# SyncE's order around the overflow branch, and how the expert rows come back into h at the end of each layer

## The chip, the cores and the metric

The kernel runs on one core of a Trainium2 chip. The metric is the device time of one execution in microseconds (us), the median of three runs. The engines are TensorE (PE, with its weight loads as PEld), VectorE (DVE), ScalarE (ACT), GpSimd (POOL) and SyncE (SP), which computes nothing and issues most transfers. Each engine runs its instructions in the order of the program; engines wait for each other and for transfers by semaphores.

## What is computed

Two layers over 512 tokens and 16 meta tokens, 1024 wide, in float32. In each layer projections feed two groups of attention heads, and a mixture of 32 experts follows, of which each token takes two. The change lies in the experts and at the layer's end:

```python
for l in range(DEPTH):                       # 2
    proj = h @ w_in[l]
    ...                                      # two head groups -> mix
    h = layer_norm(DEEPNORM_ALPHA * h + mix, ln1_g[l], ln1_b[l])
    ffn = hier_moe(h, w_grp[l], b_grp[l], w_rtr[l], b_rtr[l], w1[l], w3[l], w2[l])
    h = layer_norm(DEEPNORM_ALPHA * h + ffn, ln2_g[l], ln2_b[l])
# in hier_moe, with combine = the gate of a token for an expert, 0 where not taken:
hid = silu(einsum('td,edf->tef', t, w1)) * einsum('td,edf->tef', t, w3)
y = einsum('tef,efd->td', hid * combine[..., None], w2)
```

## The kernel before

The 528 tokens of h lie in SBUF as tiles of 128 rows, t1 to t4, and the 16 meta tokens as tile 0 (`mq`). In the traces and orders one buffer `hu` holds t1 and t2 of h, and a second one t3 and t4.

**The expert loop.** The 32 experts run as 16 pairs. A pair has six weight parts of 1 MB, four of w1 and w3 and two of w2 (`load_part`, line 311), which SP's queue loads into buffers of one rotating pool, the units. SP's transfers share eight semaphores in rotation, so a transfer waits until the one eight before it has landed. For a pair POOL gathers the rows of its tokens (xe, line 1239), PE transposes them (xtq, line 1368), ACT and DVE write them as xT (lines 1375 and 1373), PE multiplies by w1 and w3 (h, 32 matmuls), ACT and DVE make hid (lines 1322 to 1324), PE transposes it (hidT) and multiplies by w2 (yp, 16 matmuls), ACT and DVE scale yp by the gates (yw, lines 1353 and 1354), and POOL scatters yw into a table in memory, `ytab` (line 1576). The table has two halves, one for each of a token's two experts. Pairs 14 and 15 are not scattered: their rows reach h by matmuls with a selection matrix (cmb, in `combine`).

**The branch.** Ahead of pair 8 stands `overflow()`, a branch (line 1413) for experts with more tokens than their place holds. It is taken in neither layer here. Every engine passes it; SP waits there until all its transfers have landed, and POOL until all of its own have. The loop asks SP for the weights of pairs 8, 9 and 10 ahead of the branch; the units that are free allow it pair 8, pair 9 and four parts of pair 10.

**The next layer's small loads.** `begin(l + 1)` makes six loads of 0.5 to 144 KB (`gw`, `lcol`, `ng`, `alog`, `dtb`, `br`). In layer 0 it is called behind the branch. Two small operations read them soon: `eal` on ACT (line 418, from `alog`) and `hng` on DVE (line 504, from `ng`).

**The end of a layer.** In pair 15, `fetch_rows` adds the two halves of ytab to h: for each of t1 to t4 one accumulating transfer per half, on POOL (line 1517), the first halves of all tiles and then the second halves; such a transfer of one tile waits for the one before it on the same tile. Tile 0 is read plainly by SP. Then `combine` adds pairs 14 and 15: for a tile in mode "f" DVE adds the products to h (line 1403), in mode "e" PE also multiplies h by the identity (`cmb<-hu`), so that h passes through PSUM, and ACT copies it back. Mean, square (line 1623), `rs` (with a power on POOL, line 172) and the last passes (lines 1636 to 1644) are the layer norm. The steps' order is a list of words, `s` for the statistics of a tile, `n` for its norm and `t` for its transposition:

```python
NORM = "s1tf s2tf s0tf n2 n1 n0 s3epvp t1 n3 s4tf t0 t2 n4"
NORM_LAST = "s1tapp n1 s3ef s2tf n2 s4ef n3 n4"
```

In layer 0 the transposed h then feeds the projections of layer 1 (pj); in layer 1 the tiles go to the output. The order of the instructions on each engine, and of SP's transfers, comes from a scheduler which places the program's operations by due times; `tc.issue_after` holds an operation behind another.

## Time and profile before

| | before |
|---|---|
| median of 3 runs | 1440.74 us (1438.74 to 1441.36) |
| the profiled execution | 1440.8 us |
| its span in the trace | 1439.0 us |
| PE busy | 1263.3 us, 88% of the span |
| DVE, ACT, POOL busy | 770.9, 547.6, 603.3 us |
| experts of layer 0 from the branch to the last yp | some 566 to 716 us |
| end of layer 0, to the first projections | some 716 to 738 us |
| the branch of layer 1 | some 1264 to 1289 us |
| end of layer 1 | 1411 to 1439 us |

PE is busy for most of the span, so time is lost or won where PE stands idle, or where it works and nothing follows. In a timeline row the first number is the start in the span, the second how long the group of merged instructions lasted, and the bracket at the end the idle time of the engine ahead of it and what ended that. PEq, ACTq and SPq are the engines' instruction queues. Pair 8's h of layer 0 starts at 582.13, pair 9's at 610.56, pair 10's at 630.79; in layer 1 pair 8's starts at 1289.21.

### The profile page before, as it was taken

The page shows a single profiled execution, that of the slowest core. Times are in us where ns is not written, and L with a number is a line of the kernel's source. Part 1 is how long each engine was busy: PE and PEld are TensorE (multiplying, and loading weights), DVE is VectorE, ACT ScalarE, POOL GpSimd, SP SyncE. Part 2 cuts the span into 40 slices and gives each one's busy share as a digit, 9 for nine tenths or more (in the row PEclk, how much of TensorE's full clock was granted, in tenths as well). Part 3 has the DMA queues.
Part 4 walks back from the last instruction along what each step waited for, and adds up shares of the span by engine and source line. Part 5 has one row for each costly group of instructions (what it writes and reads, how often), then busy time and mean ns, then how long its engine had stood idle before and what let it go on. Part 6 is the DMA issues. An engine that isn't in the chain of part 4 may idle for free. (4 is left out here: it accounts for less than half of the span.)

```text
span 1439.0 us, 24030 instructions
## 1 busy us (share of the span) xinstructions
PE 1263.3 (88%) x8664; PEld 899.4 (63%) x8664; DVE 770.9 (54%) x2072; ACT 547.6 (38%) x1389; POOL 603.3 (42%) x791
## 2 busy tenths in 40 slices
PE   7999999899996986498879999998999789759895
PEld 6998999787884332133369988897887543213332
DVE  4887999667336111041268888997663431103114
ACT  3574544345322221122245645353553222212222
POOL 4557498745023111111255573898241131211213
PEclk9999999889997999699989999999799889978997
DMA  4252223123717999699942531222246489998995
GB/s 168 81 204 67 67 82 97 61 89 125 285 61 278 410 410 410 265 400 410 285 144 82 183 97 67 90 93 71 74 177 251 155 320 410 408 405 339 410 359 134
DMA packets 103691, 306.53 MB, mean 213 GB/s; under 512 B 24567, under 2 KB 25671, under 8 KB 103568
## 3 DMA queue, kind: packets, MB, share of 16 engines
q1 hardware_dynamic: 86160, 265.72, 48.8%
q0 software_dynamic: 11488, 26.39, 6.5%
q10 hardware_dynamic: 5920, 12.85, 2.4%
q8 instruction: 69, 1.13, 0.3%
q14 instruction: 54, 0.44, 0.1%
HBM read 281.49 MB, written 32.19 MB: 218 GB/s over the span
## 5 line engine op out<-in xcount | busy, mean ns | idle before, releaser
L226 POOL TENSOR_TENSOR wl<-wr,wh 128x256 fp32r<-128x256 f32 (+1 forms) x296 | 247.3, 865 | 193.4 <-ACT wh L221 164.4
L61 PE MATMUL h<-we,xT 128*64 128x512 f32 x1024 | 234.5, 611 | 35.5 <-ACT xT L1375 35.3
L61 PEld LDWEIGHTS h<-we,xT 128*64 128x64 f32 x1024 | 72.9, 141 | 176.0 <-issue 127.3
L61 PE MATMUL pj<-hh,wh 128*128 128x264 f32 (+2 forms) x928 | 164.6, 314 | 9.7 <-ACT raw L338 4.6
L61 PE MATMUL pj<-hl,wh 128*128 128x264 f32 (+2 forms) x928 | 160.9, 308 | 0.5 <-DVE hl L186 0.5
L61 PE MATMUL pj<-hh,wl 128*128 128x264 f32 (+2 forms) x928 | 160.1, 306 | 0.0
L61 PEld LDWEIGHTS pj<-hh,wh 128*128 128x128 f32 (+1 forms) x928 | 134.8, 196 | 17.1 <-ACT raw L338 5.4
L61 PEld LDWEIGHTS pj<-hl,wh 128*128 128x128 f32 (+1 forms) x928 | 135.4, 194 | 6.3 <-DVE hl L186 0.7
L61 PE MATMUL yp<-we,hidT 128*64 128x512 f32 x512 | 127.2, 639 | 9.6 <-ACT yw L1353 4.9
L61 PEld LDWEIGHTS pj<-hh,wl 128*128 128x128 f32 (+1 forms) x928 | 131.4, 190 | 5.0 <-issue 0.4
L221 ACT CAST wh<-wr 128x1024 fp32r<-128x1024 f32 (+1 forms) x82 | 85.4, 1044 | 101.4 <-PE pj L61 44.5
L1323 DVE SCALAR_TENSOR_TENSOR hid<-hid,h 128x256 f32<-128x256 f32 x32 | 13.5, 421 | 189.3 <-ACT hid L1322 189.3
L1576 POOL DMA_INDIRECT ytab<-yw,dest x28 | 28.1, 1003 | 190.7 <-ACT xT L1375 88.1
L1375 ACT ACTIVATE xT<-xtq,lcol 128x128 f32<-128x128 f32 x192 | 73.2, 456 | 80.9 <-PE xtq L1368 56.1
L1238 POOL MEMSET xe<- 128x1024 f32 x32 | 30.4, 951 | 167.5 <-PE h L61 146.9
L1373 DVE TENSOR_SCALAR xT<-xtq,lcol 128x128 f32<-128x128 f32 x64 | 26.2, 410 | 130.2 <-ACT xT L1375 130.2
L1322 ACT ACTIVATE hid<-h 128x256 f32<-128x256 f32 x32 | 12.3, 383 | 205.6 <-PE h L61 194.2
L61 PEld LDWEIGHTS yp<-we,hidT 128*64 128x64 f32 x512 | 35.1, 143 | 76.4 <-issue 58.7
L521 DVE SCALAR_TENSOR_TENSOR dn<-cin,cw,dn 128x528 f32<-128x528 f32 x72 | 64.8, 908 | 11.1 <-ACT dn L519 9.9
L496 DVE MATCH_REPLACE8 scores<-top,scores 128x144 f32<-128x144 f32 (+3 forms) x128 | 62.0, 487 | 0.1
L495 DVE MAX8 top<-scores 128x8 f32<-128x144 f32 (+3 forms) x128 | 60.5, 494 | 0.3
L1333 PE MATMUL hidT<-cst,hid 128*128 128x128 f32 x64 | 14.2, 305 | 39.6 <-DVE hid L1324 39.6
(431 smaller groups left out, 2434.1 us busy)
## 6 DMA issues: line engine op xcount, KB each, us to landing
we<-w SPq DMA_DIRECT2D x190, 1024.0 KB, 16.6
wr<-w_in SPq DMA_DIRECT2D x64, 512.0 KB, 3.3
wr<-w_out SPq DMA_DIRECT2D x16, 512.0 KB, 3.3
hu<-ytab POOLq DMA_DIRECT2D x16, 512.0 KB, 7.8
ytab<-zr ACTq DMA_DIRECT2D x16, 264.0 KB, 3.3
hu<-x SPq DMA_DIRECT2D x8, 512.0 KB, 3.6
hs<-hu ACTq DMA_DIRECT2D x8, 512.0 KB, 3.1
ytab<-zr ACTq DMA_DIRECT2D x16, 256.0 KB, 3.0
```

Source lines behind the costliest of these rows:

```text
L61: return nc.tensor.matmul(out, lhsT=lhsT, rhs=rhs, start=start, stop=stop)
L221: nc.scalar.copy(hi[:, :KT * m], raw)
L226: eng.tensor_tensor(lo[:, c], raw[:, c], hi[:, c], op=OP.subtract)
L495: nc.vector.max(top, sc)
L496: nc.vector.match_replace(out=sc, in_to_replace=top, in_values=sc, imm_value=GONE)
L521: nc.vector.scalar_tensor_tensor(dst, cin[:, j:j + T], cw[:, ci + j:ci + j + 1], dst, op0=OP.mult, op1=OP.add)
L1238: nc.gpsimd.memset(xe, 0.0)
L1323: nc.vector.scalar_tensor_tensor(hid, hid, 1.0, p1[:n, 0:2 * P], op0=OP.add, op1=OP.mult)
L1333: nc.tensor.transpose(p2[:, f * n:(f + 1) * n], hid[:, f * P:(f + 1) * P], ident[:n, :n])
L1373: last = nc.vector.tensor_scalar(xT[:, kk, :], src, g_, b_, op0=OP.mult, op1=OP.add)
L1375: nc.scalar.activation(xT[:, kk, :], src, AF.Identity, bias=b_, scale=g_)
L1576: nc.gpsimd.indirect_dma_start(out=ytab[:, :], out_offset=bass.IndirectOffsetOnAxis(ap=dest[:, pair:pair + 1], axis=0), in_=yw[:, :], in_o ...
```

## The change

Two things are changed.

Around pair 8, the loads of pair 8 come first, then `begin(l + 1)`, then pair 9's six parts and one of pair 10, and then the branch. Layer 1 has no next layer, so there only the number of parts that are asked for ahead of the branch changes.

At the end of each layer the first two tiles of the norm's order (t1 and t2 in layer 0, t1 and t3 in layer 1) are read from ytab by SP, plainly, into a unit for each, behind the weights of pair 15, and DVE adds both halves to h behind pair 15's h matmuls. The other two tiles (t3 and t4, and in layer 1 t2 and t4) are still added by accumulating transfers on POOL, which now stand in a chain behind a copy of one element, `come`, that reads pair 15's first part of w2.

```diff
-        def fetch_rows(t, i=None):
+        def fetch_rows(t):
             o = OFF[t] - q0
             if t:
-                if i == 0:
-                    merged[t] = unit(f"yr{t}")
-                nc.gpsimd.dma_start(h[t], ytab[i * rows + o:i * rows + o + P, :], accum_op=OP.add)
+                for i in range(2):
+                    nc.sync.dma_start(merged[t][:, i * D:(i + 1) * D], ytab[i * rows + o:i * rows + o + P, :])
...
             if pair == 8:
-                for ahead in range(3):
-                    load_pair(8 + ahead)
+                load_pair(8)
+                if l + 1 < depth:
+                    with tc.issue_after(loaded[0].ins):
+                        begun = begin(l + 1)
+                load_pair(9)
+                load_part(10, 0)
                 overflow()
-            if pair == 8 and l + 1 < depth:
-                with tc.issue_after(loaded[0].ins):
-                    begun = begin(l + 1)
...
-                with tc.issue_after(loaded[0].ins):
-                    for i in range(2):
-                        for t in norder:
-                            if t:
-                                fetch_rows(t, i)
+                whole = [t for t in norder if t]
+                for t in whole:
+                    merged[t] = unit(f"yr{t}")
+                for t in whole[:2]:
+                    fetch_rows(t)
...
+            if pair == 15:
+                come = spool.tile([P, 1], F32, name="come", bufs=1)
+                last = nc.gpsimd.tensor_copy(come[0:1], ws[4][0][0:1, 0:1])
+                for i in range(2):
+                    for t in whole[2:]:
+                        with tc.issue_after(last.ins):
+                            o = OFF[t] - q0
+                            last = nc.gpsimd.dma_start(h[t], ytab[i * rows + o:i * rows + o + P, :], accum_op=OP.add)
             hid, fed = expert_hidden(xT, lambda j: ws[j])
+            if pair == 15:
+                with tc.issue_after(fed.ins):
+                    for t in whole[:2]:
+                        for i in range(2):
+                            nc.vector.tensor_tensor(h[t], h[t], merged[t][:, i * D:(i + 1) * D], op=OP.add)
```

The scheduler then orders the instructions anew. ACT in layer 0 around the branch (`L1413`), before: the two `yw` ahead of the branch are those of pairs 6 and 7, and the `xT`, `hid` and `hidT` behind it are pair 8's.

```order
L1335 COPY hidT<-hidT 128x256
L1353 ACTIVATE yw<-yp_6380,gtab 128x512
L1353 ACTIVATE yw<-yp_6458,gtab 128x512
L1307 TENSOR_LOAD nxi
L1413 COMPARE_AND_BRANCH
...
L1375 ACTIVATE xT<-xtq,lcol 128x128 x6
L1322 ACTIVATE hid<-h_6786 128x256
L1335 COPY hidT<-hidT 128x256
L418 ACTIVATE eal<-alog 128x4
L1375 ACTIVATE xT<-xtq,lcol 128x128 x3
```

ACT at the same place in the changed kernel.

```order
L1335 COPY hidT<-hidT 128x256
L418 ACTIVATE eal<-alog 128x4
L1353 ACTIVATE yw<-yp_6380,gtab 128x512
L1353 ACTIVATE yw<-yp_6458,gtab 128x512
L1307 TENSOR_LOAD nxi
L1413 COMPARE_AND_BRANCH
...
L1375 ACTIVATE xT<-xtq,lcol 128x128 x6
L1322 ACTIVATE hid<-h_6776 128x256
L1335 COPY hidT<-hidT 128x256
L1375 ACTIVATE xT<-xtq,lcol 128x128 x3
```

`eal`, which reads one of the small loads, has moved from behind pair 8's work to ahead of the yw of pairs 6 and 7; `hng` on DVE has moved in the same way, ahead of DVE's two halves of those yw.

POOL at the end of layer 0, before: `hu_4927` holds t1 and t2, `hu_4928` t3 and t4; `wr` and `wl` are weights of the next layer's projections, `rs` belongs to the norm.

```order
L1517 DMA hu_4927<-ytab_185 128x1024 x2
L1517 DMA hu_4928<-ytab_185 128x1024 x2
L1517 DMA hu_4927<-ytab_185 128x1024 x2
L1549 MEMSET lnwq 128x512
L1517 DMA hu_4928<-ytab_185 128x1024 x2
L240 TENSOR_TENSOR wr<-gw,lcol 128x8x36
L172 TENSOR_TENSOR rs<-rs,mhalf 128x1 x2
L226 TENSOR_TENSOR wl<-wr,wh 128x232 x4
L172 TENSOR_TENSOR rs<-rs,mhalf 128x1 x2
```

POOL at the same place in the changed kernel.

```order
L1549 MEMSET lnwq 128x512
L1566 COPY come<-we_7317 1x1
L1571 DMA hu_4928<-ytab_185 128x1024 x2
L240 TENSOR_TENSOR wr<-gw,lcol 128x8x36
L172 TENSOR_TENSOR rs<-rs,mhalf 128x1
L1571 DMA hu_4928<-ytab_185 128x1024
L226 TENSOR_TENSOR wl<-wr,wh 128x232 x4
L1571 DMA hu_4928<-ytab_185 128x1024
L172 TENSOR_TENSOR rs<-rs,mhalf 128x1 x2
L226 TENSOR_TENSOR wl<-wr,wh 128x256 x4
```

The second transfer of t3 now stands behind `rs` of t1, and that of t4 behind four `L226` as well; all stood ahead of both before.

PE at the end of layer 0, before, from t0's products to the last transposes of t1 and t2 (`tp<-cst,hu_4927`):

```order
L61 MATMUL cmb<-yw,G 32x256 x16
L61 MATMUL cmb<-hu_4928,cst 128x512
L61 MATMUL cmb<-yw,G 128x512 x4
L61 MATMUL cmb<-hu_4928,cst 128x512
L61 MATMUL cmb<-yw,G 128x512 x4
L61 MATMUL fold<-sums,fold 32x1 x4
L180 MATMUL tp<-cst,hu_4927 128x128 x4
L61 MATMUL fold<-ssq,fold 32x1 x4
L180 MATMUL tp<-cst,hu_4927 128x128 x4
L61 MATMUL cmb<-yw,G 128x512 x8
L180 MATMUL tp<-cst,hu_4927 128x128 x4
L203 MATMUL tpm<-cst,mq 128x128 x2
```

PE at the same place in the changed kernel.

```order
L61 MATMUL cmb<-yw,G 32x256 x16
L61 MATMUL fold<-sums,fold 32x1 x4
L180 MATMUL tp<-cst,hu_4927 128x128 x4
L61 MATMUL fold<-ssq,fold 32x1 x4
L180 MATMUL tp<-cst,hu_4927 128x128 x4
L61 MATMUL cmb<-hu_4928,cst 128x512
L61 MATMUL cmb<-yw,G 128x512 x4
L61 MATMUL cmb<-hu_4928,cst 128x512
L61 MATMUL cmb<-yw,G 128x512 x8
L180 MATMUL tp<-cst,hu_4927 128x128 x4
L203 MATMUL tpm<-cst,mq 128x128 x2
```

The products that take t3 of h through PSUM have moved from ahead of the transposes of t1 and t2 to between them. On SP, the six small loads stand behind pair 8's weights; and in layer 1 ACT's and DVE's yw of pair 6 stands between three and three of pair 7's xT, where it stood behind six.

## Rows read from the trace of the kernel before

**Rows 1.** Timeline of PE, layer 0, pairs 8 to 10.
```profile
582.13 9.66 PE L61 MATMUL h<-we,xT 128*64 128x512 f32 x32 [11.45 <-ACT xT L1375]
...
610.56 9.10 PE L61 MATMUL h<-we,xT 128*64 128x512 f32 x32 [12.18 <-ACT xT L1375]
...
630.79 4.46 PE L61 MATMUL h<-we,xT 128*64 128x512 f32 x20
```

**Rows 2.** Timeline of POOL, the last scatter but one and the branch's end.
```profile
566.06 0.97 POOL L1576 DMA_INDIRECT ytab<-yw,dest  x1 [7.41 <-ACT yw L1353]
...
581.72 0.14 POOL L367 MEMSET sm<- 128x52 f32 x1 [6.58 <-DMA ytab<-yw,dest]
```

**Rows 3.** Timeline of ACT, pair 6's yw and `eal`.
```profile
564.85 0.69 ACT L1353 ACTIVATE yw<-yp,gtab 128x512 f32<-128x512 f32 x1
...
609.96 0.20 ACT L418 ACTIVATE eal<-alog 128x4 f32<-128x4 f32 x1 [15.87 <-DMA alog<-alog]
```

**Rows 4.** Timeline of SP's queue, two issues.
```profile
551.22 3.43 SPq L311 DMA_DIRECT2D we<-w  x1
...
604.15 0.47 SPq L153 DMA_DIRECT2D alog<-alog  x1
```

**Rows 5.** Issues from 560 and from 682 us: tile, count, size, median us to landing.
```profile
we<-w SPq DMA_DIRECT2D x4, 1024.0 KB, 21.4
...
lnw<-ln_g SPq DMA_DIRECT2D x1, 512.0 KB, 18.1
```

**Rows 6.** Timeline of PE, layer 1, pair 6's yp and pairs 8 to 10.
```profile
1259.10 3.06 PE L61 MATMUL yp<-we,hidT 128*64 128x512 f32 x8 [2.43 <-ACT yw L1353]
...
1289.21 9.40 PE L61 MATMUL h<-we,xT 128*64 128x512 f32 x32 [11.64 <-ACT xT L1375]
...
1305.13 7.09 PE L61 MATMUL h<-we,xT 128*64 128x512 f32 x32
...
1326.53 4.03 PE L61 MATMUL h<-we,xT 128*64 128x512 f32 x18
```

**Rows 7.** Timeline of POOL, end of layer 0.
```profile
724.54 0.67 POOL L240 TENSOR_TENSOR wr<-gw,lcol 128x288 f32<-128x288 f32 x1 [8.34 <-DMA wr<-w_in]
...
726.28 4.40 POOL L226 TENSOR_TENSOR wl<-wr,wh 128x232 fp32r<-128x232 f32 x4
```

**Rows 8.** Landing times on POOL's queue: lines 1517 (transfers into h), 1239 (gathers).
```profile
DMA to landing us min/median/max: 7.1/7.8/12.9
...
DMA to landing us min/median/max: 3.5/7.4/8.4
```

**Rows 9.** Timeline of PE, end of layer 0.
```profile
720.77 1.11 PE L61 MATMUL cmb<-hu,cst 128*128 128x512 f32 x2
...
723.11 1.48 PE L61 MATMUL cmb<-yw,G 128*128 128x512 f32 x4
...
737.89 2.11 PE L61 MATMUL pj<-hh,wh 128*116 128x264 f32 x8 [2.59 <-DVE hl L186]
...
746.70 1.19 PE L61 MATMUL pj<-hh,wh 128*116 128x264 f32 x8 [1.57 <-DVE hl L186]
```

**Rows 10.** Timeline of DVE, end of layer 0.
```profile
720.28 2.48 DVE L1628 SCALAR_TENSOR_TENSOR yr<-hu,mv,lnw 128x1024 f32<-128x1024 f32 x2
...
723.01 0.21 DVE L1625 TENSOR_SCALAR rs<-ssq 128x1 f32<-128x1 f32 x2
```

**Rows 11.** Timeline of ACT, the square of t3 in layer 0.
```profile
729.30 1.13 ACT L1623 ACTIVATE yr<-hu,mv 128x1024 f32<-128x1024 f32 x1
```

**Rows 12.** Timeline of PE, end of layer 1.
```profile
1413.77 2.08 PE L61 MATMUL cmb<-hu,cst 128*128 128x512 f32 x2 [2.56 <-DMA hu<-ytab]
...
1421.81 1.02 PE L61 MATMUL cmb<-hu,cst 128*128 128x512 f32 x2
```

**Rows 13.** Timeline of POOL, `rs` of t1 in layer 1.
```profile
1420.49 0.58 POOL L172 TENSOR_TENSOR rs<-rs,mhalf 128x1 f32<-128x1 f32 x1 [8.07 <-DVE rs L1625]
```

**Rows 14.** Timeline of DVE, the last pass of t4.
```profile
1433.73 1.29 DVE L1636 SCALAR_TENSOR_TENSOR hu<-yr,rs,lnw 128x1024 f32<-128x1024 f32 x1 [0.66 <-POOL rs L172]
```

## The prediction

> **What bounds the kernel now.** I read the timeline of TensorE (PE) first, since it holds the span, and in it looked for idle time; then the timelines of the engines that its waits name; then SyncE's (SP's) queue and the landings. The reader is to see three places.
>
> First the middle of layer 0's expert loop. PE stands still 11.45 us before pair 8's h and 12.18 us before pair 9's [rows 1]. The first stop is the branch: GpSimd (POOL) has two scatters still to issue, those of pairs 6 and 7, and leaves the branch when the last has landed [rows 2]. The second is ScalarE (ACT) at `eal`, which waits 15.87 us for `alog` and has pair 9's xT queued behind it [rows 3]. `alog` is late because SP's branch waits for all its weights before SP issues anything more: the load goes out at 604.15 [rows 4]. Layer 1 has the first stop alone: 11.64 us at 1289.21, and pair 9's h follows at 1305.13 without idle time [rows 6].
>
> Second the end of layer 0. Eight accumulating transfers on POOL bring ytab's rows into h; the last for t3 frees PE's `cmb<-hu` at 720.77 and the projections of layer 1 start at 737.89 [rows 9]. Third the end of layer 1, where PE waits 2.56 us for t3's last transfer [rows 12].
>
> **Part 1, the small loads ahead of the branch.** Removed: the wait at 609.96, so PE's 12.18 us before pair 9 [rows 1, 3]. Moved with it: the order puts `eal<-alog` on ACT, and `hng<-ng` on VectorE (DVE), ahead of the yw of pairs 6 and 7, where they stood behind pair 8's work. So behind the waiting instruction are now those two yw; the scatters wait for the yw, the branch for the scatters, pair 8's xT and PE for the branch.
>
> When does `alog` land? It is issued behind pair 8's last weight part, which SP issues at 551.22 [rows 4]. A weight issued in that stretch lands after 21.4 us, and a 512 KB transfer put behind weights at the end of the loop after 18.1 us [rows 5]. That is 572.6 for the part, and some 573 for the small loads behind it. Before, ACT's yw of pair 6 started at 564.85 and POOL's scatter of it at 566.06, 1.2 us later [rows 2, 3]. With yw at 573.4 it starts at about 574.6, 8.5 us later. The two scatters in a row take what they took (566.06 to 581.72 [rows 2]), so the branch ends near 590.2 and pair 8's h starts near 590.6 instead of 582.13.
>
> From there: 582.13 to 630.79 is 48.66 us, and without the 12.18 it is 36.48 [rows 1]; layer 1's same stretch, which has no such wait, takes 1326.53 - 1289.21 = 37.32 [rows 6]. Pair 10's h then starts at 627.1 or 627.9 where it was 630.79. If pair 9's h also runs at layer 1's 7.09 instead of 9.10 [rows 1, 6], 2.0 us come off. And if the loads land after 18.1 and not 21.4, the hold is 3.3 shorter. Bounds -9.0 and -2.9; I take **-3.7 us**, since the 21.4 is of the same stretch. Of what else moves: the six loads take six of the eight places of SP's rotating semaphores, so pair 9's weights go out later. I put this at nothing; the cover is that pair 8's h itself is 8.5 us late and pair 9's comes 16 us behind it (1289.21 to 1305.13 [rows 6]); if both were used up, PE would wait for pair 9's weights at a microsecond for each. Behind the branch SP has six issues fewer, which helps weights that are in time already: nothing.
>
> In layer 1 only the yw moves, ahead of three of pair 7's xT: PE's wait of 2.43 at 1259.10 [rows 6] gets shorter by at most that. **-0.5 us**, bounds -0.9 and 0.
>
> The Trainium skill (DMA: Bandwidth & Descriptors, Anatomy of one DMA) fits a transfer issued from GpSimd by a fixed cost near 2.0 us plus its bytes over 436 GB/s. As an estimate by that, `alog` would land 2 us behind its issue and hold nobody. The trace speaks against it: 18.1 us behind weights, and 5.8 even after the branch [rows 3 to 5]. It is rival A below.
>
> **Part 2, the end of layer 0.** Four of POOL's eight transfers go; SP reads t1's and t2's rows plainly behind pair 15's weights, and DVE adds them, 1.24 us each by the nearest row, two-input passes over the same 128x1024, two in 2.48 [rows 10]. SP's reads wait for pair 13's scatter and hold the ln2 rows behind them; the norm reads those only from 720.28 [rows 10], so that costs nothing. POOL's copy `come` holds the other four transfers until a weight of pair 15 is there, ahead of anything that needs them: nothing. The first add fits in front of DVE's second yw pass. The other three stand ahead of t1's rs, which DVE wrote at 723.01 [rows 10]: 3 x 1.24 = 3.7 later is 726.7, or 725.5 because one of the two passes that stood ahead of it now stands behind. I take 726.2. POOL waits with t1's `L172` for this. It was held until then by the wr load, 8.34 us at 724.54 [rows 7]; that load now goes out earlier, as POOL's memset no longer stands behind six transfers, and the wait goes, but rs takes its place.
>
> Behind that `L172` stands t3's second transfer, which had landed by 720.77 before. It is now issued near 726.8. Its landing: 7.1 at least and 7.8 at the median with two more in flight [rows 8]; alone, as here, the nearest row is a gather of the same queue, 3.5 at best [rows 8]. I take the middle, 5.6, so 732.4; bounds 730.3 and 734.6. PE's `cmb<-hu` of t3 stands ahead of t2's transposes in the new order, and the projections need those. From `cmb<-hu` of t3 to the end of its products it is 3.8 us (720.77 to 724.59 [rows 9]), about 1.1 for the copy to h and the mean, then t3's square on ACT and the casts of t1 and t2 behind it: from that square to the first projection it was 737.89 - 729.30 = 8.6 [rows 9, 11], with waits in it; the square and five casts alone are near 4.3. Sum 9.2 to 13.5, I take 11: the projections start at 743.4 (bounds 739.5 and 748.1) where they started at 737.89, **+5.5 us** (+1.6 to +10.2). t4's second transfer is behind four more `L226`, 4.40 us [rows 7]: issued near 732.1, landed by 740 at 7.8; its half of the projections comes 8.8 us after the first (746.70 [rows 9]), so it is not later than the first half makes it.
>
> The Trainium skill (SBUF — State Buffer, Terms) says that VectorE and GpSimd take a shared pair of ports by turns, each for a whole instruction. No row of these groups shows what that costs here. As an estimate, one add in the way of t3's transfer would make the sum 1.3 us longer.
>
> **Part 3, the end of layer 1.** t1 and t3 are read and added by DVE, so PE's 2.56 us at 1413.77 goes [rows 12], and the first of t3's products, about 1.1 us, no longer delays t1's: `L172` of t1 comes near 1416.8 instead of 1420.49 [rows 13]. t4's second transfer is behind that `L172`: issued 1417.4, landed 1420.9 to 1425.2 by the same bounds, where its `cmb<-hu` stood at 1421.81 [rows 12]. From there to the start of t4's last pass at 1433.73 [rows 14] it was 11.9 us, with POOL's and DVE's passes for the other tiles in the way; these are now done earlier. The chain alone, by the durations of layer 0, is 3.8 of products, 1.1 for copy and mean, 1.3 of square and some 1.5 for rs on DVE and POOL: 7.7. A landing at 1423 then gives 1430.7, and the bounds 1428.6 and 1432.9. **-3.0 us**, bounds -5 and, if the other tiles' passes stay in the way, 0.
>
> **Sum:** the times of each part are in the clock of the kernel before, and the parts follow each other, so they add: -3.7 - 0.5 + 5.5 - 3.0 = -1.7 against the profiled execution's 1440.8 us, whose span is 1439.0; the median of the runs is 1440.74, so nothing is to be shifted: 1439.1.
>
> **The rivals.** *A, the small loads land early* (they pass the weights, as after the branch, 5.8 us from issue): nobody is held, the second stop goes whole, -12.2 instead of -3.7, so 1430.6. For it: layer 1 shows that the stop needn't be. Against it: the 18.1 and 21.4 us behind weights [rows 5]. Chance 0.14. *B, slower: t3's second transfer is slow.* Now that it stands alone behind `L172`, every microsecond of its landing is PE's. The slowest of the sixteen took 12.9 [rows 8]. With that the projections start at 739.7 + 11 = 750.7, +12.8, and the sum is +5.6: 1446.4. It decides from a landing of about 10.2 us, where the sum passes +2.9. Layer 1's wr loads share the transfers at that time; against it speaks that the 12.9 was one of three issued at once. With the other ways to the upper bound of part 2, 0.24. *C, the change does not reach the end of layer 0*: the projections' start is set by t1's and t2's casts as before and t3 has slack. The +5.5 falls away: 1433.6. For it: 17 us lay between t3's `cmb<-hu` and the projections [rows 9]. Against it: the new order. 0.12.
>
> **How the numbers follow.** My forecast has 0.50, with a spread from its bounds of about 4 us to either side: of it 0.15 faster by over 0.2% (2.9 us, about what a measurement of this kernel can tell from no change), 0.30 within, 0.05 slower. A and C are faster, 0.26. B is slower for 0.22, and 0.02 within. Faster 0.41, same 0.32, slower 0.27. The range goes from A's 1431 to B's 1447, with 0.1 on either side beyond.
>
> **What would show it.** Right: in the changed kernel ACT's `eal` waits near 564.8 for `alog` until 572 to 574, PE's idle time before pair 8's h is near 20 us counted with pair 7's yp, and there is none before pair 9's; pair 10's h starts near 627; the projections of layer 1 start 5 to 6 us later than that alone would give, behind t3's `cmb<-hu`; PE has no wait for t3 at the end of layer 1. Wrong: `alog` in before 566 (A), the landing of t3's second transfer beyond 10 us (B), a start of the projections unmoved against the last yp (C).

## The result, and the profile after

The changed kernel takes 1431.17 us (median of 20 runs, 1428.82 to 1436.33) against 1440.09 us of the kernel before on the same chip (20 runs, 1433.15 to 1446.09): ratio 0.9938, 95% interval 0.9925 to 0.9952, or 8.9 us less, 7 to 11 by the interval. Two later comparisons gave 0.9939 (0.9918 to 0.9961) and 0.9950 (0.9928 to 0.9972). The forecast was faster by 1.7 us. The direction holds; four fifths of the gain were not foreseen.

| | before | after |
|---|---|---|
| the profiled execution's span | 1439.0 us | 1428.9 us |
| PE busy | 1263.3 us | 1260.8 us |
| DVE, ACT, POOL busy | 770.9, 547.6, 603.3 us | 779.9, 548.1, 595.1 us |
| pair 7's h to pair 10's h, layer 0 | 75.16 us | 68.48 us |
| pair 15's h to the first projection, layer 0 | 37.65 us | 42.22 us |
| pair 0's h to pair 10's h, layer 1 | 166.26 us | 160.64 us |
| pair 15's h to the end, layer 1 | 42.98 us | 41.45 us |

In the changed kernel line 1576 of before (the scatter) is 1590, 1517 has become 1571 (transfers into h) and 1516 (plain reads), 1625 (rs) is 1639, and 1636 (the last pass) is 1650.

**The branch of layer 0.** PE's timeline of the changed kernel, pairs 8 to 10, which answers to [rows 1]:

```profile
591.13 9.14 PE L61 MATMUL h<-we,xT 128*64 128x512 f32 x32 [11.90 <-ACT xT L1375]
...
606.80 7.09 PE L61 MATMUL h<-we,xT 128*64 128x512 f32 x32
...
625.03 5.32 PE L61 MATMUL h<-we,xT 128*64 128x512 f32 x24
```

The wait of 12.18 us before pair 9 is gone, pair 8 starts 9.0 us later, pair 10 is 5.76 us earlier. ACT's and POOL's timelines of the same place, against [rows 2, 3]:

```profile
571.82 0.20 ACT L418 ACTIVATE eal<-alog 128x4 f32<-128x4 f32 x1 [5.33 <-DMA alog<-alog]
571.94 0.67 ACT L1353 ACTIVATE yw<-yp,gtab 128x512 f32<-128x512 f32 x1
```

```profile
573.32 0.97 POOL L1590 DMA_INDIRECT ytab<-yw,dest  x1 [14.81 <-DVEq L1413]
582.03 0.97 POOL L1590 DMA_INDIRECT ytab<-yw,dest  x1 [7.74 <-DMA ytab<-yw,dest]
590.73 0.14 POOL L367 MEMSET sm<- 128x52 f32 x1 [7.72 <-DMA ytab<-yw,dest]
```

`eal` waits for `alog`, the yw of pair 6 stands behind it, the two scatters follow one another, and the branch ends 9.0 us later than before: the chain of the forecast, link by link.

**The end of layer 0.** POOL's and PE's timelines, against [rows 7, 9]:

```profile
692.92 1.91 POOL L1571 DMA_DIRECT2D hu<-ytab  x2 [0.20 <-issue]
714.72 1.23 POOL L240 TENSOR_TENSOR wr<-gw,lcol 128x288 f32<-128x288 f32 x1 [19.89 <-DMA wr<-w_in]
718.44 0.82 POOL L172 TENSOR_TENSOR rs<-rs,mhalf 128x1 f32<-128x1 f32 x1 [2.48 <-DVE rs L1639]
719.23 0.87 POOL L1571 DMA_DIRECT2D hu<-ytab  x1
```

```profile
724.57 2.08 PE L61 MATMUL cmb<-hu,cst 128*128 128x512 f32 x2 [0.52 <-DMA hu<-ytab]
...
736.72 2.08 PE L61 MATMUL pj<-hh,wh 128*116 128x264 f32 x8 [2.33 <-DVE hl L186]
```

The second transfer of t3 goes out 0.8 us behind t1's `L172`, and PE takes t3 5.3 us later, the moment it is there. From that to the projections it is 12.15 us. The chain is as foreseen, but not each of its links: POOL's wait for the wr load has not gone (19.89 us, until 714.72), and rs, which does end last, is 23.9 us behind pair 15's h, where 26 had been forecast (726.2 against 700.25).

**The end of layer 1.** POOL's and PE's timelines, against [rows 12, 13]:

```profile
1408.06 0.58 POOL L172 TENSOR_TENSOR rs<-rs,mhalf 128x1 f32<-128x1 f32 x1 [6.58 <-DVE rs L1639]
1408.64 0.90 POOL L1571 DMA_DIRECT2D hu<-ytab  x1
```

```profile
1405.71 1.12 PE L61 MATMUL cmb<-hu,cst 128*128 128x512 f32 x2 [1.38 <-DVE hu L1577]
...
1414.05 1.60 PE L61 MATMUL cmb<-hu,cst 128*128 128x512 f32 x2 [2.65 <-DMA hu<-ytab]
```

PE's wait for t3's transfer is gone (1.38 us for DVE's adds in its place), and t4's second transfer, behind `L172`, now has a wait of 2.65 us.

**What was not in the forecast.** The windows of the expert loop of layer 1 from pair 0's h to pair 10's h (columns: the window, its length, busy time of PE, PEld, DVE, ACT and POOL, then the granted clock, the DMA engines' busy share and GB/s), first the kernel before, then the changed one:

```profile
1160.27:1326.53 166.26, 136.65 (x604) 47.99 (x606) 34.44 (x67) 41.10 (x99) 32.42 (x33) 0.91 0.98 387
```

```profile
1157.37:1318.01 160.64, 129.62 (x605) 45.76 (x607) 32.34 (x65) 40.86 (x99) 32.38 (x33) 0.94 0.98 386
```

The matmuls are the same (604 and 605 of them) and PE is busy 7.0 us less, at a higher granted clock, 0.94 against 0.91. This stretch is 5.6 of the 10.1 us between the two spans. Whether the change brings that about is asked at the end.

### The profile page after: what moved, and what is told of

Read it like the earlier page. It is cut to its first block, busy times and chain, and to the rows that moved or that the text cites. A ratio compares the mean times of both kernels' runs of the same rounds, so it can differ in the third digit from the quotient of the medians.

```text
span 1428.9 us, 24040 instructions
## 1 busy us (share of the span) xinstructions
PE 1260.8 (88%) x8664; PEld 897.9 (63%) x8664; DVE 779.9 (55%) x2080; ACT 548.1 (38%) x1389; POOL 595.1 (42%) x785
## 5 line engine op out<-in xcount | busy, mean ns | idle before, releaser
L226 POOL TENSOR_TENSOR wl<-wr,wh 128x256 fp32r<-128x256 f32 (+1 forms) x296 | 246.2, 864 | 196.1 <-ACT wh L221 172.6
L61 PE MATMUL pj<-hl,wh 128*128 128x264 f32 (+2 forms) x928 | 161.5, 308 | 0.3 <-DVE hl L186 0.3
L521 DVE SCALAR_TENSOR_TENSOR dn<-cin,cw,dn 128x528 f32<-128x528 f32 x72 | 64.8, 909 | 10.2 <-ACT dn L519 9.1
```

The source lines that it names most:

```text
L61: return nc.tensor.matmul(out, lhsT=lhsT, rhs=rhs, start=start, stop=stop)
L226: eng.tensor_tensor(lo[:, c], raw[:, c], hi[:, c], op=OP.subtract)
L521: nc.vector.scalar_tensor_tensor(dst, cin[:, j:j + T], cw[:, ci + j:ci + j + 1], dst, op0=OP.mult, op1=OP.add)
```

## Experiments

One trace of each kernel can't be read to better than some 3 us in a stretch: two traces of the kernel before differ by that and more. So the stretches of all traces are put together here. Each is the difference of the starts of two groups in PE's timeline; "order" tells whether the kernel has the changed order around the branch, "new end" in which layers two tiles are read plainly. A ratio is that of the timed runs to those of the kernel before on the same chip.

| kernel | order | new end | ratio (95% interval) | layer 0, h of pair 7 to 10 | layer 0, h of pair 15 to projections | layer 1, h of pair 0 to 10 | its clock | layer 1, h of pair 15 to end |
|---|---|---|---|---|---|---|---|---|
| before | old | none | 1 | 75.16 | 37.65 | 166.26 | 0.91 | 42.98 |
| before_again | old | none | one run | 72.66 | 36.57 | 163.19 | 0.93 | 48.42 |
| ends_only | old | both | 0.9982 (0.9965 to 0.9998) | 72.64 | 40.36 | 165.77 | 0.91 | 40.20 |
| order_only | new | none | 0.9964 (0.9947 to 0.9980) | 69.45 | 39.73 | 160.20 | 0.94 | 47.82 |
| after | new | both | 0.9938 (0.9925 to 0.9952) | 68.48 | 42.22 | 160.64 | 0.94 | 41.45 |
| after_again | new | both | 0.9939 (0.9918 to 0.9961) | 69.52 | 40.19 | 160.51 | 0.94 | 41.49 |
| after_third | new | both | 0.9950 (0.9928 to 0.9972) | 68.12 | 42.25 | 160.30 | 0.94 | 41.66 |
| held | new, `eal` held | both | 0.9933 (0.9912 to 0.9953) | 64.88 | 43.25 | 160.72 | 0.94 | 41.59 |
| end1_only | new | layer 1 | 0.9945 (0.9924 to 0.9967) | 72.97 | 36.07 | 160.23 | 0.94 | 41.60 |
| end1_again | new | layer 1 | 0.9934 (0.9908 to 0.9960) | 66.89 | 38.13 | 161.93 | 0.93 | 39.79 |
| hold8 | new | none; layer 1 held | 0.9935 (0.9911 to 0.9958) | 72.90 | 35.77 | 162.11 | 0.93 | 44.16 |
| nocome | new | both, no hold | 0.9982 (0.9959 to 1.0004) | 70.50 | 35.76 | 160.99 | 0.94 | 44.46 |
| held_end1 | new, `eal` held | layer 1 | 0.9928 (0.9905 to 0.9950) | 60.44 | 46.36 | 163.66 | 0.92 | 41.19 |
| front_rs | new | both, issued earlier | 0.9963 (0.9942 to 0.9984) | 72.89 | 41.80 | 161.50 | 0.94 | 39.34 |

### The two parts apart

`order_only` has only the hunk at pair 8, `ends_only` only the rest; `before_again` is the kernel before, unchanged. From the changed kernel to `order_only`:

```diff
-                for t in whole[:2]:
-                    fetch_rows(t)
+                with tc.issue_after(loaded[0].ins):
+                    for i in range(2):
+                        for t in norder:
+                            if t:
+                                fetch_rows(t, i)
...
-                with tc.issue_after(fed.ins):
-                    for t in whole[:2]:
-                        for i in range(2):
-                            nc.vector.tensor_tensor(h[t], h[t], merged[t][:, i * D:(i + 1) * D], op=OP.add)
```

And `ends_only`:

```diff
-                load_pair(8)
...
-                load_part(10, 0)
+                for ahead in range(3):
+                    load_pair(8 + ahead)
```

Expected of `order_only`:

> Only the order around pair 8 is changed (small loads ahead of pair 9's weights, then the branch); both layer ends are those of the kernel before. In the changed kernel's trace pair 10's h of layer 0 starts 5.8 us earlier than before and that is what this run should keep. Theory 1 (what is gained beyond that belongs to neither part and comes from how the clock dipped in the profiled executions): 5 to 7 us faster than before, 1433 to 1435. Theory 2 (layer 1's stretch gains 6 us because the order of layer 1's instructions moved with the loads): 11 to 13 us faster, 1427 to 1429. Theory 3 (the extra belongs to the ends): as theory 1, and the ends alone show it.

Expected of `ends_only`:

> Only the two layer ends are changed; the order around pair 8 is that of the kernel before. From the two traces the end of layer 0 lost 5.4 us and the end of layer 1 won 1.6. Theory 1 and 2: about 3.8 us slower than before, 1443 to 1445. Theory 3: 2 to 3 us faster, 1437 to 1438, with layer 1's expert stretch or attention shorter by some 6 us against before.

Expected of `before_again`:

> The kernel before once more, for a second trace: by how much the starts at fixed places (pair 10's h of layer 0, the first projections of layer 1, pair 0's yp and pairs 7, 8 and 10 of layer 1) differ between two executions of one kernel. Theory 1 expects differences of 3 us and more in layer 1's attention and experts, theories 2 and 3 less than 1.5 us.

Measured: `order_only` 1437.21 us and `ends_only` 1440.63 us beside 1442.64 us (23 runs) of the kernel before; `before_again` 1440.87 in its one run. The order alone gives -5.2 us (-7.6 to -2.9), the ends alone -2.6 us (-5.0 to -0.3). By its terms the forecast had the order at -3.7 - 0.5 = -4.2 and the ends at +5.5 - 3.0 = +2.5. So the order was sized well, and **the ends have the other sign**. The time of `ends_only` is that of theory 3, without its condition: its loop of layer 1 takes 165.77 us, as in the kernel before. The two traces of the kernel before differ by 3.1 us in that loop and by 5.4 at the end of layer 1.

Their traces show why. In `order_only` PE reaches pair 15 of layer 1 at 1383.15, 12.8 us earlier than in the profile of before, and the kernel ends only 8.0 earlier. PE's timeline of `order_only`, yp of pair 15:

```profile
1395.60 3.68 PE L61 MATMUL yp<-we,hidT 128*64 128x512 f32 x8 [3.53 <-DMA we<-w]
1402.91 3.32 PE L61 MATMUL yp<-we,hidT 128*64 128x512 f32 x8 [3.63 <-DMA we<-w]
```

PE waits for the last weights, which the kernel before had in time. POOL's timeline of `order_only` at the same time:

```profile
1388.32 0.88 POOL L1517 DMA_DIRECT2D hu<-ytab  x1 [6.10 <-issue]
1392.14 0.85 POOL L1517 DMA_DIRECT2D hu<-ytab  x1 [2.95 <-issue]
1396.02 0.86 POOL L1517 DMA_DIRECT2D hu<-ytab  x1 [3.03 <-issue]
1399.86 0.84 POOL L1517 DMA_DIRECT2D hu<-ytab  x1 [2.98 <-issue]
```

The old end's transfers go out among the weights, one in 3.8 us. Two windows that hold such a stretch, `order_only` with the transfers among the weights and the changed kernel with the transfers held until 1391.7:

```profile
1385.00:1403.00 18.00, 9.45 (x38) 2.70 (x36) 1.59 (x3) 1.44 (x3) 3.44 (x4) 0.81 1.05 255
```

```profile
1380.00:1398.00 18.00, 14.86 (x68) 5.56 (x70) 6.01 (x10) 4.70 (x11) 2.05 (x3) 0.98 1.04 389
```

The DMA engines are busy all the time in both, and move 255 GB/s in the one and 389 in the other. The packets of the first window, by queue, show which transfers take the time (q0 holds POOL's accumulating transfers alone there, q1 SP's loads; packets, MB, share of the 16 engines' time):

```profile
q0 software_dynamic: 758, 2.76, 78.4%
q1 hardware_dynamic: 493, 1.83, 26.9%
```

A megabyte of the accumulating transfers takes 28% of the window, one of SP's loads 15%. In `before_again` there is a second form of it: pair 15 is 5.4 us earlier than in the profile of before and the end is not earlier at all, since PE then waits 7.44 us for t3's rows. So the old end has no price of its own: what PE gains ahead of it the transfers take back, in part or whole.

### The hold and the halving of the transfers apart

`nocome` takes the hold away (in both layers); `hold8` keeps the old end in layer 0, and in layer 1 adds all four tiles by eight transfers, held behind `come`; `end1_only` has the new end in layer 1 and the old one in layer 0; `after_again` is the changed kernel. From the changed kernel to `nocome`:

```diff
-                last = nc.gpsimd.tensor_copy(come[0:1], ws[4][0][0:1, 0:1])
+                last = loaded[0]
```

To `end1_only` (in `hold8` `nw` is 0 in both layers, and `come` is read in layer 1 as here):

```diff
-                for t in whole[:2]:
+                nw = 2 if l + 1 == depth else 0
+                for t in whole[:nw]:
...
-                last = nc.gpsimd.tensor_copy(come[0:1], ws[4][0][0:1, 0:1])
+                last = nc.gpsimd.tensor_copy(come[0:1], ws[4][0][0:1, 0:1]) if nw else loaded[0]
...
-                    for t in whole[2:]:
+                    for t in whole[nw:]:
...
```

Expected of `nocome`:

> The changed kernel without the copy that holds the four transfers: they start as soon as pair 13's scatter has landed, and the scheduler then puts all four ahead of rs in layer 0. Theory (the hold only matters through the place of t3's second transfer): the end of layer 0 gets 4 to 5 us shorter, the end of layer 1 stays, 4 to 5 us faster than the changed kernel. Rival (the hold is what keeps the last weights in time): the second half of pair 15's yp waits for its weight, 3 us or more in layer 1, and the gain is 0 to 2 us.

Expected of `hold8`:

> The order around the branch as changed, layer 0's end as before, and in layer 1 all eight transfers on POOL as before, but held behind the copy that reads pair 15's first part of w2. Against the run with the order alone this differs only by the hold. Theory (the gain at the end of layer 1 comes from fewer transfers: eight of them take 2.5 to 3.8 us each of the transfer engines, one behind the other): pair 15's yp no longer waits for weights, but the last transfer lands as late as before or later, from pair 15's h to the end 47 us or more, no faster than the order alone. Rival (the hold alone gives it): from pair 15's h to the end 41 to 43 us, 5 us faster than the order alone.

Expected of `end1_only`:

> The changed kernel with the end of layer 0 as it was before (eight transfers, none held), the order around the branch and the end of layer 1 as changed. From pair 15's h to layer 1's first projections the kernel before took 37.6 and 36.6 us in two traces, the changed kernel 42.2. Theory (the new end of layer 0 costs 4 to 5.5 us, because t3's second transfer stands behind rs): 4 to 5 us faster than the changed kernel. Rival (PE arrives earlier, so the eight transfers and the last weights share the transfer engines and the old end costs about the same): within 1.5 us of the changed kernel.

Expected of `after_again`:

> The changed kernel once more beside these, for its second trace and for its time on the same chip. Both theories: 0.993 to 0.995 of the kernel before; from pair 15's h to layer 1's first projections 41 to 43 us, from pair 15's h of layer 1 to the end 40 to 42 us.

Measured beside 1439.69 us (22 runs) of the kernel before: `nocome` 1438.32, `hold8` 1432.22, `end1_only` 1431.49, `after_again` 1430.88. Of the end of layer 1: 46.4 us in the mean of the three traces with the old end, 44.16 with the hold alone, 44.46 with the halving alone, 41.1 with both (mean of eight). In the traces, one of each, either gives some 2 of the 5.3 us, and either leaves a wait; the three traces with the old end differ by more than that among themselves (42.98 to 48.42). PE's timeline of `hold8`, where eight transfers stand behind the hold, and of `nocome`, where the four go out among the last weights and reads:

```profile
1409.06 2.08 PE L61 MATMUL cmb<-hu,cst 128*128 128x512 f32 x2 [7.63 <-DMA hu<-ytab]
```

```profile
1414.73 2.07 PE L61 MATMUL cmb<-hu,cst 128*128 128x512 f32 x2 [4.68 <-DVE hu L1577]
```

In `hold8`, behind the weights, the fourth to the eighth transfer go out 2.5 us apart (1396.91, 1399.39, 1401.86, 1404.39, 1406.86) where they took 3.8 among them.

The times do not share it out evenly. `hold8` and `end1_only` differ by the halving in layer 1 alone, and by 0.7 us, which is nothing to be told. `nocome`, which has the halving and not the hold, is 7.4 us slower than the changed kernel. So in the time the hold is what counts, and no gain of the halving is seen. Neither theory on `nocome` came out whole. For `hold8` the trace lies between theory and rival (44.16 us, where 47 or more and 41 to 43 were expected), and the time is on the rival's side.

`nocome` also tells what the end of layer 0 costs. There the halved transfers stand ahead of t1's rs again. POOL's timeline of `nocome`:

```profile
707.33 0.87 POOL L1571 DMA_DIRECT2D hu<-ytab  x1 [8.51 <-DMA hu<-ytab]
711.18 0.86 POOL L1571 DMA_DIRECT2D hu<-ytab  x1 [2.98 <-DMA lnw<-ln_g]
...
721.14 0.82 POOL L240 TENSOR_TENSOR wr<-gw,lcol 128x288 f32<-128x288 f32 x1 [8.56 <-DMA wr<-w_in]
724.44 0.82 POOL L172 TENSOR_TENSOR rs<-rs,mhalf 128x1 f32<-128x1 f32 x1 [2.48 <-DVE rs L1639]
```

The second transfers go out 17 and 13 us ahead of `L172`, and that end takes 35.76 us, no more than the old one (37.3 in the mean of six, without `held_end1`). So in this trace the reading and adding by DVE cost the end of layer 0 nothing; what is left as the cause of its longer end is the place behind rs that the hold brought with it.

The times don't follow these traces elsewhere either. `nocome` is 0.4% slower than the changed kernel, while its trace is 5.8 us shorter at the end of layer 0 than the mean of the three of the changed kernel (41.6) and 2.9 longer at the end of layer 1 (41.5); the rest of it (424.2 us from the first projection to pair 0's h of layer 1, against 420.3 to 421.0) is one trace's, and it is not settled. And `end1_only`, without the cost at the end of layer 0, takes as long as the changed kernel.

### The small loads' readers held

`held` puts `eal` and `hng` behind pair 9's hid, so that no yw stands behind `alog`; `at9` holds those two operations, on ACT and on DVE.

```diff
-        nc.scalar.activation(eal, alog, AF.Exp)
+        with tc.issue_after(at9[0].ins) if at9 else contextlib.nullcontext(): nc.scalar.activation(eal, alog, AF.Exp)
...
-        nc.vector.tensor_scalar(hng, ng, 0.5, None, op0=OP.mult)
+        with tc.issue_after(at9[1].ins) if at9 else contextlib.nullcontext(): nc.vector.tensor_scalar(hng, ng, 0.5, None, op0=OP.mult)
```

> The changed kernel with eal and hng put behind pair 9's hid, nothing else moved: the small loads stay ahead of the branch, but nobody waits for them ahead of it. If the wait at eal costs what the traces show (the branch of layer 0 ends 9.0 us later than before), pair 8's h starts near 582 again, the stop before pair 9 stays away, and this is about 8 to 9 us faster than the changed kernel: 1422 to 1424. Rival: pair 9's weights, which are issued later now, become what pair 9's h waits for, and only 3 to 5 us are won: 1426 to 1428.

Measured: 1432.59 us beside 1442.64, ratio 0.9933, not to be told from the changed kernel, where 3 to 9 us less were expected. Pair 8's h starts at 582.82, as before the change, and there is no stop at `eal`. But PE's timeline of `held` has a new wait inside pair 9's h, and ACT's timeline shows from where:

```profile
603.74 3.65 PE L61 MATMUL h<-we,xT 128*64 128x512 f32 x16 [2.13 <-ACT xT L1375]
```

```profile
602.65 0.69 ACT L1353 ACTIVATE yw<-yp,gtab 128x512 f32<-128x512 f32 x1 [7.75 <-SPq L1413]
```

Behind `eal` stood a second gate: the first yw after the branch waits for SP to pass it. The pairs 7 to 10 take 64.9 us, 3.8 less than in the mean of the changed kernel's three traces (68.7), where the removed wait of 9 us at the first stop had promised more. The gate is 2.13 us of the rest. Another 3.2 go with the granted clock in the stretch from the end of pair 9's h to pair 10's h. The same stretch of `held_end1` (below) shows it, where the gate opens earlier and PE does not wait (first `held` at 0.64, then `held_end1` at 0.85):

```profile
607.40:621.66 14.26, 13.82 (x34) 5.02 (x36) 10.90 (x13) 6.19 (x14) 1.97 (x2) 0.64 1.02 408
```

```profile
606.40:617.51 11.11, 10.68 (x37) 3.65 (x36) 8.77 (x11) 5.83 (x14) 1.97 (x2) 0.85 1.03 416
```

### A version that was to beat both

`held_end1` is `end1_only` with the hold of `eal` and `hng`; `end1_again` and `after_third` are two of the kernels above once more on the same chip.

Expected of `held_end1`:

> The order around layer 0's branch and the new end of layer 1 as in the change; the end of layer 0 as before; and the two small operations that read the small loads (eal on ACT, hng on DVE) are held behind pair 9's hid, so that no yw waits for alog. Theory (each of the three places is worth in the time what it is worth in the traces): pair 7's h to pair 10's h of layer 0 takes about 65 us (68.5 to 69.5 in the changed kernel, 64.9 where the hold alone was tried), the end of layer 0 about 36 us from pair 15's h to the first projection (40.2 to 42.2 in the changed kernel), the end of layer 1 41.5 us as there. Together 7 us less: 1424. Rival 1 (the attention of layer 1 and the branch of layer 1 take back what comes early, since they wait for weight loads that set their own pace): the two stretches are shorter in the trace as said, the ones behind them longer, and the time is within 2 us of the changed kernel's 1431. Rival 2 (the second gate of ACT's and DVE's yw of pair 8, the wait for SP's branch, costs more in some executions): h07 to h10 of 70 and more.

Expected of `end1_again`:

> The kernel with the changed order and the new end of layer 1 alone, once more, with the changed kernel beside it on the same chip and more rounds, because its trace had 36.1 us at the end of layer 0 against 40.2 to 42.2, and its median did not show this. Theory (the new end of layer 0 costs 4 to 5 us): 3 to 5 us faster than the changed kernel. Rival (the stretch behind gives it back: the attention of layer 1 waits for something that is not late because of the end of layer 0): within 1 us of the changed kernel, and the stretch from the first projection to pair 0's h of layer 1 longer by some 4 us.

Expected of `after_third`:

> The changed kernel again, nothing edited, beside the two others on the same chip: 1431 us, end of layer 0 some 41 us, end of layer 1 some 41.5 us from pair 15's h, and pair 0's yp of layer 1 at 3.65 us if the granted clock is full there as in the other traces of the changed order (5.35 us in the kernel before).

Measured beside 1443.55 us (18 runs): `held_end1` 1431.74, `end1_again` 1434.26, `after_third` 1435.98. The first two are 4.2 and 1.7 us below the changed kernel, with intervals that overlap its own, where 7 and 3 to 5 were expected: it is not told that either is faster. Pairs 7 to 10 of `held_end1` take 60.44 us, 8 less than in the changed kernel, but the end of layer 0 takes 46.36. PE's timeline of `held_end1` in layer 0, yp of pair 15:

```profile
698.70 3.68 PE L61 MATMUL yp<-we,hidT 128*64 128x512 f32 x8 [2.80 <-DMA we<-w]
705.99 3.68 PE L61 MATMUL yp<-we,hidT 128*64 128x512 f32 x8 [3.61 <-DMA we<-w]
```

This is what `order_only` showed in layer 1. The window of it (690 to 706 us), `held_end1` first, then `held`, which has the same order around the branch and holds the transfers until 694.4:

```profile
690.00:706.00 16.00, 8.19 (x32) 2.24 (x28) 1.59 (x3) 1.45 (x3) 3.98 (x5) 0.71 1.05 259
```

```profile
690.00:706.00 16.00, 13.80 (x61) 5.05 (x60) 4.63 (x8) 3.05 (x7) 2.09 (x3) 1.00 1.00 326
```

Rival 1 of that expectation is right in its sum, in another place than it named: what PE wins in the middle of the loop meets the transfers and the last weights at its end. In `end1_again` the stretch behind the end of layer 0 took 423.4 us, in `end1_only` 417.8: what the end of layer 0 is worth in the time stays open.

`front_rs` moves the second transfers of the changed kernel ahead of the rs.

```diff
-            with tc.issue_after(done.ins), tc.issue_after(last_read.ins):
+            with tc.issue_after(done.ins), tc.issue_after(last_read.ins), tc.issue_after(last.ins):
                 begun += (weights(l + 1, 32, MISC, extra=begun[:2]),)
...
-            held[1] = rpow(rs[:, c], rs[:, c], mhalf, 1)
+            with tc.issue_after(last.ins) if t == whole[0] else contextlib.nullcontext(): held[1] = rpow(rs[:, c], rs[:, c], mhalf, 1)
```

> The changed kernel with one thing moved: on GpSimd the second transfers of the two tiles that are added by transfers stand ahead of the rs of the norm's first tile (and in layer 0 ahead of the wr product of line 240), where in the changed kernel they stand behind it. In the changed kernel's trace GpSimd stood idle there for 19.9 us, waiting for the wr load, while t3's first transfer had long landed. Theory (t3's second transfer behind rs is the cost of the new end of layer 0, and PE's 2.65 us wait for hu at the end of layer 1 has the same cause): from pair 15's h to the first projection 36 to 38 us in layer 0 instead of 40.2 to 42.2, from pair 15's h to the end 39 to 40 us in layer 1 instead of 41.5, and a time 4 to 6 us below the changed kernel's 1431 to 1436. Rival 1 (the start of the projections is set by the norm of t1 and t2, as rival C of the prediction had it): no change at the end of layer 0, within 2 us of the changed kernel. Rival 2 (the second transfers, now issued near 701, fall among SP's plain reads, the ln2 rows and the wr loads, and make these late): the wr load of 714.7 lands some microseconds later and the projections start as late as before or later.

Measured: 1437.78 us beside 1443.63 (17 runs), ratio 0.9963 (0.9942 to 0.9984), against 0.9938 to 0.9950 of the changed kernel: no gain. In layer 1 the theory holds, 39.34 us (39 to 40 expected) and no wait for t4. In layer 0 it takes 41.80 us instead of 36 to 38. POOL's and ACT's timelines:

```profile
709.92 0.87 POOL L1571 DMA_DIRECT2D hu<-ytab  x1 [8.67 <-DMA hu<-ytab]
727.94 0.58 POOL L172 TENSOR_TENSOR rs<-rs,mhalf 128x1 f32<-128x1 f32 x1 [17.16 <-DVE rs L1639]
```

```profile
737.41 1.05 ACT L221 CAST wh<-wr 128x1024 fp32r<-128x1024 f32 x1 [3.64 <-DMA wr<-w_in]
738.37 0.59 ACT L1401 ACTIVATE hu<-cmb 128x512 f32<-128x512 f32 x1
```

Only one second transfer now goes out ahead of the first rs, by 18 us; the other still stands behind an `L172`, at 728.52. And the edit also moved the next wr loads: in SP's queue the second one stood ahead of the stores of t1 and went out at 712.39, here it stands behind the first of them and goes out at 731.75. ACT's cast waits for it with t3's copy to h behind it. One wait was traded for another, near rival 2, but the wr load of the cast was late by its place in SP's queue. So in layer 0 this run speaks neither for nor against the reading of `nocome`; it is one more edit whose hold moved more than was meant.

## Why the prediction was right and wrong

**The total: the way is right, the size is not.** 1431.17 us lies inside the range of the forecast, 1431 to 1447, but at its very end, and that end was the price of rival A, which did not happen: this is luck. Of the 7.2 us that were missing, by the timed runs of the two parts, some 5 lie in the ends (-2.6 where +2.5 was forecast) and 1 in the order (-5.2 where -4.2 was), which is inside its interval.

**The branch of layer 0: right.** Forecast -3.7 us (bounds -9.0 and -2.9). In the mean of three traces with the old order pairs 7 to 10 take 73.5 us, of nine with the new one (without `held` and `held_end1`) 70.2: -3.3. `alog` held `eal` until 571.8 where 573 was forecast, pair 8's h started at 591.1 (590.6 forecast), pair 10's at 625.0 (627.1 forecast); the 2.1 us between are pair 9's h at 7.09, which the forecast had named and left in the bounds.

**Rival A fell.** The loads don't pass the weights: from its issue at 559.78 to the end of `eal`'s wait `alog` took 12.0 us. By the fit of the Trainium skill (DMA: Bandwidth & Descriptors, Anatomy of one DMA), which is for a transfer that GpSimd issues, it would as an estimate have been there in some 2 us; this trace, where SP issues it behind weights, does not agree. The rival's price of -12.2 is not refuted: with nobody held by `eal`, pairs 7 to 10 take 64.9 us in `held` and 60.4 in `held_end1`, 8.6 and 13.0 less than the mean with the old order. SP's branch, the second gate, took some of it in the first and none in the second.

**The yw of layer 1: the mechanism right, worth nothing.** PE's wait of 2.43 us before pair 6's yp [rows 6] is gone in the changed kernel and in `held`, and pair 7's h comes earlier; but PE's stop before pair 8 grows from 11.64 to 15.05 us. PE's timeline of the changed kernel:

```profile
1249.13 1.94 PE L61 MATMUL yp<-we,hidT 128*64 128x512 f32 x8
...
1284.24 6.04 PE L61 MATMUL h<-we,xT 128*64 128x512 f32 x18 [15.05 <-ACT xT L1375]
```

From pair 0's h to pair 10's the three traces of the changed kernel take 160.3 to 160.6 us, `order_only` and `end1_only`, where the yw stayed behind six xT and this gain at pair 7 is missing, 160.2.

**The end of layer 0: right.** Forecast +5.5 us (+1.6 to +10.2); means of 41.7 us in five traces with the new end (`ends_only`, `held` and the changed kernel's three) and 37.3 in six with the old one: +4.3. In the changed kernel the landing took 5.3 us (5.6 taken), from t3's `cmb<-hu` to the projections it was 12.2 us (11 taken), and rs came some 2 us sooner behind pair 15's h than taken, so that errors of either sign cancel. Rival C fell with this; rival B's slow landing did not come: the transfers that go out by themselves behind `L172` are with PE 5.3 us later in layer 0 (719.23 to 724.57) and 5.4 in layer 1 (1408.64 to 1414.05). In the measured time this cost is not resolved, as said.

**The end of layer 1: mis-sized, the step that failed.** Forecast -3.0 us (-5 to 0). Against the profile that stood ahead of the forecast it is -1.5 (42.98 to 41.45), with the chain as forecast: `L172` 5.8 us behind the last yp (6.0), PE has t4 5.4 us behind its issue, 9.7 us from t4's `cmb<-hu` to its last pass (7.7 taken, 11.9 before). But the means are 46.4 and 41.1, **-5.3**. The step that failed is "the parts follow each other, so they add": the old end was priced at one arrival of PE, and it grows when PE comes earlier, as `before_again` and `order_only` show. Each end was read from one trace, and this one happened to be the shortest of the three. This is 2.3 of the 3.5 us by which the two ends together (4.3 - 5.3 = -1.0 in the traces) differ from their forecast of +2.5; the timed -2.6, with an interval of -5.0 to -0.3, agrees with the traces in sign.

**The granted clock of layer 1: taken as constant, which it is not.** "The times of each part are in the clock of the kernel before" took for granted that the clock of a stretch stays. Over 14 traces the loop of layer 1, pairs 0 to 10, goes by it: 0.91: 166.3 and 165.8; 0.92: 163.7; 0.93: 163.2, 161.9 and 162.1; 0.94: 160.2 to 161.5. The three traces with the old order have 165.1 in the mean, the eleven with the new one 161.2: **-3.9 us**, while the one move that the change makes there, the yw's, gains nothing by itself. The steps can be found: pair 0's yp, the same 16 matmuls, takes 5.35 us in both traces of the kernel before and 3.65 in all three of the changed kernel; the granted clock in it is 0.68 in the first trace of the one and 1.00 in that of the other.

That the change brings this about is not shown, and the record speaks rather against it. The two groups overlap (163.2 in `before_again`, 163.7 in `held_end1`). The slow yp of pair 0 also stands in `end1_again` and `hold8`, which have the new order, and not in `ends_only`, which has the old one. And the granted clock of whole executions, which is on record for the runs of the experiments, is no higher in the changed kernel: 0.9387 in the mean of `after_again` (7 runs) and 0.9368 of `after_third` (12), beside 0.9385 (22) and 0.9373 (18) of the kernel before. A rise from 0.91 to 0.94 in 160 of 1430 us would make some 0.003 of this; that is an estimate from these lengths.

The four together, -3.3 + 4.3 - 3.9 - 5.3 = -8.2, come near the -8.9 timed, but with the third term in doubt this proves nothing; without it they are -4.3. The other stretches differ by 1 to 4 us from trace to trace, of the same kernel too, and are left out. Where the rest of the gain comes from stays open.

## What to carry to other kernels

A term that is read at one arrival of the waiting engine holds for that arrival alone: before summing the parts, ask for each later stretch what sets its end when the stretch ahead gets shorter (here the stream of weights, and transfers that go out among it). Transfers that aren't needed until the last loads are in should be held behind them: here `hold8`, which only holds them, is not to be told in its time from `end1_only`, which also halves their number, while `nocome`, which only halves it, is slower than the changed kernel. A hold that is put into a queue moves what stands behind it: look at who comes next in that queue, as the rs of POOL here, the wr loads of SP in `front_rs`, and SP's branch behind `alog`.

## What the runs showed of the hardware

An accumulating transfer of 512 KB takes far more of the DMA engines than its bytes say. With such transfers among the weights the engines were busy all the time (1.05) and moved 255 and 259 GB/s, and 389 and 326 in windows of the same length and place in the loop that hold only the first two of them. Where they stood among weights, 2.76 MB of them took 78% of the engines' time and 1.83 MB of loads 27%. One transfer followed the other in 3.8 us among weights and in 2.5 us behind them, and one by itself landed in 5.3 us.

The granted clock of a loop that runs the same matmuls over the same data was 0.91 to 0.94 of full speed in different traces, of one kernel too (0.91 and 0.93), and the loop took 166.3 to 160.2 us.
